# Second feed-forward of a kernel of two transformer blocks: down-projection pieces braided with block pieces of later chunks

## The chip, the cores and the metric

The kernel runs on one core of one Trainium2 chip. Its time is the device time of one launch in microseconds. TensorE (PE) multiplies, VectorE (DVE) and ScalarE (ACT) work elementwise, GpSimd (POOL) does little here, and SyncE (SP) issues the loads.

## The reference, cut to what matters

Two transformer blocks run one after the other on x of 256 tokens by 2048 columns, in float32. The parts that the change touches:

```python
# first block, attention (16 heads, 128 + 64 columns each); the 64 rope columns of k are shared by all heads
q = concat([q[..., :128], apply_rope(q[..., 128:], positions)])
k = concat([k[..., :128], apply_rope(k[..., 128:], positions)])
attn = causal_block_attention(q, k, v)
...
# first block, feed-forward, D_FF = 5632
h2 = rmsnorm(x, ffn_norm_g)
x = x + (silu(h2 @ w_ffn_gate) * (h2 @ w_ffn_up)) @ w_ffn_down
...
# second block, feed-forward, D_FF_2 = 8192
h2 = rms_norm(x, g_ff)
x = x + jnp.square(jax.nn.relu(h2 @ w_ff1)) @ w_ff2
```

## The kernel before

All matrix products run in a split form: an operand is cut into a high part that TensorE takes exactly and a low rest, and a product is three matmuls (high by high, low by high, high by low). Activations are split once and stay in SBUF. Weights come in **pieces** of 512 KB: 256 rows by 512 columns (two k tiles). The function `drive` walks a list of jobs in program order. For each piece it places a load on SP into a raw slot (L197), a cast to the high part on ACT (L230), a subtraction for the low part on DVE (L232), and the piece's matmuls on PE. Casts and subtractions are placed up to `AHEAD` pieces before the matmuls (4 for a PLAIN piece, 3 for MIX and STR), as far as a slot of W for the two parts is free: 6 slots for PLAIN pieces, 3 for MIX, 2 for STR. A load may be issued when the piece that had its raw slot before is split. Each engine runs its instructions in the order in which they were placed, SP too.

A **plain piece** (`chunk`, L262 to L264) is 12 matmuls of 512 columns: 2 k tiles by 2 token tiles by 3. A **block piece** (`strassen`, kind STR, L315 to L317) computes the same product of 2 by 2 blocks from seven block products instead of eight: 21 matmuls of 256 columns. It needs three weight sums beforehand, made on DVE in the raw slot (`sums`, L207 to L209, called L223 to L225 in the kernel after), placed two pieces before the split. Its seven products lie in PSUM banks 0 to 3, and `fin` combines them at the end of a chunk (ACT L328, DVE L329 to L332). Raw slots before: R has 4 for plain pieces of all kinds, G has 3 for block pieces.

Stages in order: the first block's projections and attention (`t_pair` transposes q and k of a pair of heads, `s_pair` makes the scores), its output projection (`wide`, three calls; `transposed_s` transposes the result and forms its block sums), the first feed-forward in three groups (11 gate chunks of plain pieces, each braided with an up chunk of block pieces, and after each group the down chunks), the second block, and the second feed-forward. There, 16 chunks of ff1 (512 columns each, 8 pieces) alternate plain and block: a plain and a block chunk are braided (pieces p p s p s p s p s p s p s p s s), and after each second braid come 32 plain down pieces over 16 k tiles. `ends` applies relu and square to a block chunk (ACT), `t_a` transposes a chunk (PE) and splits it (ACT L378, DVE L379), `ev_acc` adds a down result to x (DVE, L907; L953 after).

Of the kernel before, what the change touches and what calls it, by code (L numbers as in the profile page):

```python
# [24 lines left out]
RAWS = 3  # L25
# [46 lines left out]
def body(tc, d, out):  # L72
# [4 lines left out]
    with tc.manual_schedule(), \  # L77
# [82 lines left out]
        def drive():  # L160
# [3 lines left out]
            seen_h, seen_r, cnt = {}, {}, {}  # L164
            for i, j in enumerate(pcs):
                kind = j[5]

                def cells(s):
                    a, b, w = hslots(s)
                    return [(o + x) // 256 for o in (a, b) for x in range(0, w, 256)]  # L170

                last, s = min((max(seen_h.get(x, -1) for x in cells(s)), s) for s in SLOTS[kind])
                num.append(s)
                free_h.append(last)
                seen_h.update((x, i) for x in cells(s))
                rk = kind == STR
                m = cnt.get(("r", rk), 0)
                cnt[("r", rk)] = m + 1
                slot = (rk, m % (RAWS if rk else RAW))
                rnum.append(slot[1])  # L180
                free_r.append(seen_r.get(slot, -1))
                seen_r[slot] = i
            raws, hl, used = {}, {}, [-1]
            nd, nt, ns = [0], [0], [0]

            def dma():
                while nd[0] < len(pcs) and free_r[nd[0]] < ns[0] and nd[0] < ns[0] + 2 * RAW:
                    i = nd[0]
                    if i in before_dma:
                        before_dma[i]()  # L190
                    src = pcs[i][1]
                    a, n = src.shape[1], src.shape[2]
                    if pcs[i][5] == STR:
                        t = G[:, 2048 + 2048 * rnum[i] : 4096 + 2048 * rnum[i]]
                    else:
                        t = R[:, 1024 * rnum[i] : 1024 * rnum[i] + 1024]
                    sync.dma_start(t[:, : a * n].rearrange("p (a b) -> p a b", a=a), src)  # L197
                    raws[i] = t
                    nd[0] += 1

            def sums(upto):

                while nt[0] <= min(upto, nd[0] - 1):
                    i = nt[0]
                    if pcs[i][5] == STR:
                        v = raws[i].rearrange("p (a b) -> p a b", a=8)
                        dve.tensor_tensor(v[:, 4:6, :], v[:, 0:4:3, :], v[:, 1::-1, :], op=ALU.subtract)  # L207
                        dve.tensor_tensor(v[:, 6, :], v[:, 3, :], v[:, 4, :], op=ALU.subtract)  # L208
                        dve.tensor_tensor(v[:, 7, :], v[:, 2, :], v[:, 6, :], op=ALU.subtract)  # L209
                    nt[0] += 1  # L210

            def split(upto):
                while ns[0] <= min(upto, len(pcs) - 1) and free_h[ns[0]] <= used[0]:
# [9 lines left out]
                    if kind == STR:  # L223
                        n, a = 1792, 7
                        t = t[:, 256:]  # L225
# [16 lines left out]
            for j in jobs:  # L242
                if j[0] == "run":
                    j[1]()
                else:
                    split(k + AHEAD[j[5]])
                    assert ns[0] > k
                    j[2](*hl.pop(k))
                    used[0] = k
                    k += 1  # L250

# [44 lines left out]
        def strassen(pair, forms, w, kts, c0, evict, later=False):  # L296
# [3 lines left out]
            prod = [(("x", 0, 0), 0, 2, 1), (("x", 1, 0), 1, 0, 0), (("s", 3), 2, 3, 0), (("x", 1, 1), 6, 2, 0),  # L300
                    (("s", 0), 3, 1, 1), (("s", 1), 5, 0, 1), (("s", 2), 4, 1, 0)]

            def mk(j):
                def fn(h, l):
                    opened = set()
                    for x, wi, bank, half in prod:
                        o = PS[:, bank * 512 + half * QW : bank * 512 + (half + 1) * QW]
                        if x[0] == "x":
                            xh, xl = pair(2 * j + x[1], x[2])
                        else:  # L310
                            xh, xl = forms[:, 0, j, x[1], :], forms[:, 1, j, x[1], :]
                        first = j == 0 and bank not in opened
                        opened.add(bank)
                        last = j == kts // 2 - 1
                        pe.matmul(o, xh, h[:, wi, :], start=first, stop=False, skip_group_check=True)  # L315
                        pe.matmul(o, xl, h[:, wi, :], start=False, stop=False, skip_group_check=True)  # L316
                        pe.matmul(o, xh, l[:, wi, :], start=False, stop=last, skip_group_check=True)  # L317
                return fn

            for j in range(kts // 2):  # L320
                items.append(piece(wsrc(w, 2 * j, c0, 512), mk(j), kind=STR))

            def fin():
                q = PS[:, 0:2048].rearrange("p (a b) -> p a b", a=8)
                u = rview(G, 1024, 4, QW)
# [3 lines left out]
                dve.tensor_tensor(u[:, 0:2, :], v[:, 0:1, :].to_broadcast(bc), q[:, 0:2, :], op=ALU.add)  # L329
                dve.tensor_tensor(u[:, 2:4, :], u[:, 1:2, :].to_broadcast(bc), q[:, 2:4, :], op=ALU.add)  # L330
                dve.tensor_tensor(v[:, ::-1, :], u[:, 2:3, :].to_broadcast(bc), q[:, 3:5, :], op=ALU.add)
                dve.tensor_tensor(u[:, 3, :], u[:, 3, :], q[:, 6, :], op=ALU.add)  # L332
                if not later:
                    ends()

            def ends():
                evict(0, rview(G, 1024, 4, QW)[:, 0:4:3, :])
# [5 lines left out]
        def braid(a, b, inject=None):  # L343

            pa, pb = [x for x in a if x[0] == "pc"], [x for x in b if x[0] == "pc"]
            order = [pa[0], pa[1]]
            for i in range(6):
                order += [pb[i], pa[i + 2]]
            order += [a[-1], pb[6], pb[7], b[-1]]
            for at in sorted(inject or {}, reverse=True):  # L350
                order.insert(at, ("run", inject[at]))
            return order

        def transposed_s(nat, pair, forms, kts, gain):

            x4, s4 = rview(G, 0, 2, 2, NT, P), rview(G, 1024, 2, 4, P)
# [319 lines left out]
        qkT = rview(B, 4096, 2, 6, S)  # L676
        pT = [rview(B, 4096 + 3072, 2, 512), rview(C, 2048, 2, 512)]
# [5 lines left out]
        def zero_pT():  # L683
            for t in pT:
                pool.memset(t[:, :, 0:P].bitcast(F32), 0.0)

# [34 lines left out]
        def t_pair(p):  # L721
# [12 lines left out]
            split2(qkT[:, 0, 4:6, :], qkT[:, 1, 4:6, :], bank.rearrange("p (a b) -> p a b", a=2))  # L734

        def s_pair(p):
            rq = rqs[p % 2]
            banks = []
            for h in range(2):
                bank = aux_tile()  # L740
                banks.append(bank)
                for qt in range(NT):
# [3 lines left out]
                    hp = slice(64 * h, 64 * h + 64)  # L746
                    mm3(o, [qkT[hp, i, 4, qs] for i in range(2)], [qkT[hp, i, 5, :] for i in range(2)], False, True)
# [91 lines left out]
        def wide(pair, w, ev, tr, pending, kts=16, inject=None, row0=0, last=PLAIN):  # L839

            for c in range(4):
                inj = dict(inject or {}) if c == 0 else {}
                if pending is not None:
# [4 lines left out]
                                  kind=last if c == 3 else PLAIN))  # L848
# [65 lines left out]
        for gi, (c0, nch) in enumerate(groups):  # L914
            aT = pairat(B, 0, 16)
            for j in range(nch):
                c = c0 + j
                jobs.extend(braid(chunk(h2T, "w_ffn_gate", KT, c * 512, 512, ev_silu, kind=MIX, fixed=(4, 5)),
# [279 lines left out]
        def half(tok, i):  # L1198

            v = rview(G, 1024, 4, QW)[:, 0:4:3, :] if tok == 0 else tmp.rearrange("p (a b) -> p a b", a=2)  # L1200
# [10 lines left out]
        pending = {4: pending}  # L1211
        for gi in range(4):
            aT = pairat(B, 0, 16)
            for j in range(0, 4, 2):
                c = 4 * gi + j
                plain = chunk(h2T, "w_ff1_2", KT, c * 512, 512, lambda tok, ps: relu2(abuf[:, tok, :], tok, ps),
                              kind=MIX, fixed=(4, 5))
                block, ends = strassen(h2T, h2F, "w_ff1_2", KT, (c + 1) * 512, lambda tok, v: relu2(v, tok, v), later=True)
                jobs.extend(braid(plain, block, pending))
                pending = {1: t_a(aT, blocks(abuf), j), 2: ends, 7: t_a(aT, half, j + 1)}  # L1220
            for oc in range(4):
                inj = None
                if oc == 0:
                    inj = {1: pending[2], 2: pending[1], 4: pending[7]}
                    pending = None
                ev = ev_out(oc) if gi == 3 else ev_acc(oc)
                jobs.extend(chunk(aT, "w_ff2_2", 16, oc * 512, 512, ev, row0=16 * gi, inject=inj,
                                  kind=MIX, fixed=DOWN[oc]))


# [17 lines left out]
def blockwise(name, c):  # L1248

    return name == "w_ffn_up" or (name == "w_ff1_2" and c % 2 == 1)  # L1250
# [62 lines left out]
```

## Time and profile before

| | us |
|---|---|
| time before, median of 3 runs (lowest, highest) | 2721.99 (2720.91, 2722.18) |
| time of the profiled execution | 2722.61 |
| its span, first to last instruction | 2720.9 |

The profile is of one core at full granted clock. Busy time of an engine is given as a share of the span; a matmul's duration in the profile overlaps the next one's, so that the distance from one start to the next is what a matmul costs.

### The profile page before, as it was taken

How to read it: one execution, taken by the hardware profiler on the slowest of the kernel's cores; microseconds unless marked ns; L12 is line 12 of the kernel's file. 1: busy time of each engine (PE TensorE's matmuls, PEld its weight loads, DVE VectorE, ACT ScalarE, POOL GpSimd, SP SyncE). 2: the span in 40 equal slices, each digit the busy share in tenths (PEclk: the TensorE clock that was granted, in tenths of full speed). 3: DMA queues.
4: the chain of work that ended last, by engine and by line, in shares of the span. 5: the costliest groups of instructions: out<-in, count | busy, mean ns of one | idle time of the engine just before them, and what ended most of it. 6: DMA issues, size and time to landing. Idle time of an engine off the chain costs nothing. (4 is left out here: it accounts for less than half of the span.)

```text
span 2720.9 us, 35965 instructions
## 1 busy us (share of the span) xinstructions
PE 2709.6 (100%) x13996; PEld 2278.4 (84%) x13996; DVE 1851.8 (68%) x2233; ACT 1402.6 (52%) x1749; POOL 73.0 (3%) x153
## 2 busy tenths in 40 slices
PE   9999999999999999999999999999999999999999
PEld 8988888888888888888888888888888888898887
DVE  6555667766996699579755565455678486685774
ACT  6544666545654455345455555544556355464553
POOL 1000111000000000000000010000000000000000
PEclk9999999999999999999999999999999999999999
DMA  7666534554555555565555554555555555655555
GB/s 255 212 212 201 168 127 146 177 180 172 200 187 179 202 206 186 180 210 185 177 196 172 192 183 166 188 188 181 173 180 182 190 200 177 208 179 185 209 176 164
DMA packets 143179, 506.66 MB, mean 186 GB/s; under 512 B 16160, under 2 KB 18592, under 8 KB 142496
## 3 DMA queue, kind: packets, MB, share of 16 engines
q1 hardware_dynamic: 142864, 504.31, 54.8%
q8 instruction: 109, 1.79, 0.3%
q14 instruction: 62, 0.51, 0.1%
q10 hardware_dynamic: 144, 0.05, 0.0%
HBM read 502.21 MB, written 2.10 MB: 185 GB/s over the span
## 5 line engine op out<-in xcount | busy, mean ns | idle before, releaser
L232 DVE TENSOR_TENSOR W<-R,W 128x1024 fp32r<-128x1024 f32 (+2 forms) x795 | 943.5, 1208 | 508.8 <-ACT W L230 505.4
L230 ACT CAST W<-R 128x1024 fp32r<-128x1024 f32 (+2 forms) x798 | 810.7, 1035 | 532.1 <-PE PS L264 445.1
L263 PE MATMUL PS<-W,A 128*128 128x512 f32 (+2 forms) x1728 | 677.8, 392 | 3.2 <-DVE W L232 3.1
L262 PE MATMUL PS<-W,A 128*128 128x512 f32 (+2 forms) x1728 | 678.5, 393 | 0.6 <-ACT W L230 0.4
L264 PE MATMUL PS<-W,A 128*128 128x512 f32 (+2 forms) x1728 | 675.8, 391 | 0.0
L262 PE MATMUL PS<-W,B 128*128 128x512 f32 (+1 forms) x1248 | 492.0, 394 | 0.0
L263 PE MATMUL PS<-W,B 128*128 128x512 f32 (+1 forms) x1248 | 489.4, 392 | 0.9 <-DVE W L232 0.9
L264 PE MATMUL PS<-W,B 128*128 128x512 f32 (+1 forms) x1248 | 489.3, 392 | 0.0
L230 ACT CAST W<-G 128x1792 fp32r<-128x1792 f32 x152 | 257.5, 1694 | 304.7 <-PE PS L316 173.6
L264 PEld LDWEIGHTS PS<-W,A 128*128 128x128 f32 x1728 | 323.9, 187 | 73.7
L263 PEld LDWEIGHTS PS<-W,A 128*128 128x128 f32 x1728 | 324.4, 188 | 72.5 <-DVE W L232 6.6
L262 PEld LDWEIGHTS PS<-W,A 128*128 128x128 f32 x1728 | 324.2, 188 | 68.3 <-ACT W L230 0.8
L232 DVE TENSOR_TENSOR W<-G,W 128x1792 fp32r<-128x1792 f32 x152 | 307.0, 2020 | 40.6 <-ACT W L230 40.6
L263 PEld LDWEIGHTS PS<-W,B 128*128 128x128 f32 x1248 | 234.1, 188 | 54.6 <-DVE W L232 1.8
L264 PEld LDWEIGHTS PS<-W,B 128*128 128x128 f32 x1248 | 233.9, 187 | 54.2
L262 PEld LDWEIGHTS PS<-W,B 128*128 128x128 f32 x1248 | 234.0, 188 | 53.7
L317 PE MATMUL PS<-W,C 128*128 128x256 f32 x608 | 169.8, 279 | 0.0
L315 PE MATMUL PS<-W,C 128*128 128x256 f32 x608 | 169.8, 279 | 0.0
L316 PE MATMUL PS<-W,C 128*128 128x256 f32 x608 | 169.4, 279 | 0.0
L315 PE MATMUL PS<-W,A 128*128 128x256 f32 x456 | 128.6, 282 | 0.0
L317 PE MATMUL PS<-W,A 128*128 128x256 f32 x456 | 127.3, 279 | 0.8 <-DVE W L232 0.8
L316 PE MATMUL PS<-W,A 128*128 128x256 f32 x456 | 127.3, 279 | 0.0
(231 smaller groups left out, 2481.5 us busy)
## 6 DMA issues: line engine op xcount, KB each, us to landing
R<-in_w_in_dram SPq DMA_DIRECT2D x224, 512.0 KB, 4.5
R<-in_w_ff_dram SPq DMA_DIRECT2D x192, 512.0 KB, 3.6
R<-in_w_ffn_gate_dram SPq DMA_DIRECT2D x88, 512.0 KB, 4.4
G<-in_w_ffn_up_dram SPq DMA_DIRECT2D x88, 512.0 KB, 3.5
R<-in_w_ffn_down_dram SPq DMA_DIRECT2D x88, 512.0 KB, 3.5
R<-in_w_out_dram SPq DMA_DIRECT2D x64, 512.0 KB, 4.3
G<-in_w_ff_dram SPq DMA_DIRECT2D x64, 512.0 KB, 3.5
R<-in_w_attn_o_dram SPq DMA_DIRECT2D x32, 512.0 KB, 4.2
```

The source lines that it names most:

```text
L230: act.copy(hv, v)
L232: dve.tensor_tensor(lv, v, hv.bitcast(F32), op=ALU.subtract)
L262: pe.matmul(o, x[0], w[0], start=first, stop=False)
L263: pe.matmul(o, x[0], w[1], start=False, stop=False)
L264: pe.matmul(o, x[1], w[0], start=False, stop=last)
L315: pe.matmul(o, xh, h[:, wi, :], start=first, stop=False, skip_group_check=True)
L316: pe.matmul(o, xl, h[:, wi, :], start=False, stop=False, skip_group_check=True)
L317: pe.matmul(o, xh, l[:, wi, :], start=False, stop=last, skip_group_check=True)
```

## The change

Five parts. (1) In the second feed-forward only ff1 chunks 0 and 1 are plain; chunks 2 to 15 are block chunks. Chunk 1 is braided with chunk 2. Each of chunks 3 to 15 is braided with 8 down pieces of earlier chunks, in the pattern p p s p s p s s twice, so that `down` is cut into 32 chunks over 8 k tiles instead of 16 over 16. Of each such ff1 chunk the piece j = 4 is `flat`: eight products of 256 columns, as a MIX piece, without sums. That makes 99 block pieces for 64. (2) `sums` handles two block pieces in one set of three instructions where the two stand at most six pieces apart and the load of the second has been placed; otherwise one. (3) G has four raw slots of 1792 columns, two neighbours for a pair; `fin`'s result and `transposed_s`'s sums move from G to the last quarter of R, so that MIX pieces have three raw slots (PLAIN pieces four). (4) In `wide`'s calls that end in MIX, chunks 1 to 3 are MIX, not chunk 3 alone. (5) The rope part of the scores is contracted over 128 rows: the k rows of the other head are zeros in two copies of k.

```diff
@@ drive
+RSLOTS = {0: range(4), 1: range(3)}
...
+                if kind == STR:
+                    blocks_at.append(i)
+                    r = 4 + (len(blocks_at) - 1) % 4
+                else:
+                    r = min((seen_r.get(x, -1), x) for x in RSLOTS[kind])[1]
...
+            mate = {}
+            for a, b in zip(blocks_at[0::2], blocks_at[1::2]):
+                if b - a <= 6:
+                    mate[a] = b
@@ sums
-                    if pcs[i][5] == STR:
-                        v = raws[i].rearrange("p (a b) -> p a b", a=8)
-                        dve.tensor_tensor(v[:, 4:6, :], v[:, 0:4:3, :], v[:, 1::-1, :], op=ALU.subtract)
...
+                    if pcs[i][5] == STR and i not in summed:
+                        n = 2 if i in mate else 1
+                        if n == 2:
+                            if mate[i] < nd[0]:
+                                summed.add(mate[i])
+                            elif i > ns[0]:
+                                return
+                            else:
+                                n = 1
+                        o = 1024 + 1792 * (rnum[i] - 4)
+                        v = G[:, o : o + 1792 * n].rearrange("p (c a b) -> p c a b", c=n, a=7)
+                        dve.tensor_tensor(v[:, :, 4:6, :], v[:, :, 0:4:3, :], v[:, :, 1::-1, :], op=ALU.subtract)
+                        dve.tensor_tensor(v[:, :, 6, :], v[:, :, 3, :], v[:, :, 4, :], op=ALU.subtract)
+                        dve.tensor_tensor(v[:, :, 0, :], v[:, :, 2, :], v[:, :, 6, :], op=ALU.subtract)
@@ strassen
+                def flat_fn(h, l):
+                    h, l = (t.rearrange("p a (b c) -> p (a b) c", b=2) for t in (h, l))
+                    for kt, tok, wi, bank, half in flat:
+                        three(at(bank, half), pair(2 * j + kt, tok), h[:, wi, :], l[:, wi, :], False,
+                              (bank, half) == (3, 1) and kt == 1 and j == max(plain))
@@ the order of pieces
+        BRAID, HALF = "ppspspspspspspss", "ppspspss" * 2
@@ t_pair and s_pair
-            split2(qkT[:, 0, 4:6, :], qkT[:, 1, 4:6, :], bank.rearrange("p (a b) -> p a b", a=2))
+            split2(qkT[:, 0, 4, :], qkT[:, 1, 4, :], bank[:, 0:S])
+            for h in range(2):
+                hp = slice(64 * h, 64 * h + 64)
+                split2(qkT[hp, 0, 5 + h, :], qkT[hp, 1, 5 + h, :], bank[hp, S:])
...
-                    mm3(o, [qkT[hp, i, 4, qs] for i in range(2)], [qkT[hp, i, 5, :] for i in range(2)], False, True)
+                    mm3(o, [qkT[:, i, 4, qs] for i in range(2)], [qkT[:, i, 5 + h, :] for i in range(2)], False, True)
@@ wide
-                                  kind=last if c == 3 else PLAIN))
+                                  kind=last if c else PLAIN))
@@ second feed-forward
+        def down(g, oc, fixed):
+            at = 8 * (g % 2)
+            return chunk(Pair(aT.v[:, :, at : at + 8, :]), "w_ff2_2", 8, oc * 512, 512, (ev_out if g == 7 else ev_acc)(oc),
+                         row0=8 * g, kind=MIX, fixed=fixed)
...
+        jobs.extend(at_pieces(ff1(0), {3: pending}))
+        block, ends = ff1_blocks(2)
+        jobs.extend(merge(BRAID, ff1(1), block, {3: t_c(0, blocks(abuf))}))
+        pending = {1: t_c(1, blocks(abuf)), 2: ends, 7: t_c(2, half)}
+        for c in range(3, 16):
+            g, o = (c - 3) // 2, 2 * ((c - 3) % 2)
+            block, ends = ff1_blocks(c, (4,))
+            jobs.extend(merge(HALF, down(g, o, (4, 5)) + down(g, o + 1, (4, 5)), block, pending))
+            pending = {2: ends, 7: t_c(c, half)}
```

**Place 1, DVE in the second feed-forward.** In the rows below W<-R is the subtraction of a plain or flat piece, W<-G that of a block piece, and G<-G with 512 and 256 elements are the sums; DMAHW numbers name the load that a row waits for. Before, in a braid:

```order
L232 TENSOR_TENSOR W<-R,W 128x1024 [waits DMAHW3_49,Activation_49]
L207 TENSOR_TENSOR G<-G 128x512 [waits DMAHW6_49]
L208 TENSOR_TENSOR G<-G 128x256 [waits DVE_49]
L209 TENSOR_TENSOR G<-G 128x256 [waits DVE_49]
L232 TENSOR_TENSOR W<-G,W 128x1792 [waits PE_49,Activation_49]
L232 TENSOR_TENSOR W<-R,W 128x1024 [waits DMAHW5_49,Activation_49]
```

After, in a loop of an odd chunk, from the first down chunk's result (L953, behind piece n5) on; L419 is the transposed chunk's split:

```order
L953 TENSOR_TENSOR X<-X,PS 128x512 [waits PE_49] x2
L247 TENSOR_TENSOR W<-R,W 128x1024 [waits DMAHW3_49,Activation_49]
L419 TENSOR_TENSOR B<-PS,B 128x512 [waits Activation_49] x2
L223 TENSOR_TENSOR G<-G 128x2x512 [waits DMAHW6_49,DMAHW0_49]
L224 TENSOR_TENSOR G<-G 128x2x256 [waits DVE_49]
L225 TENSOR_TENSOR G<-G 128x2x256 [waits DVE_49]
L247 TENSOR_TENSOR W<-R,W 128x1024 [waits DMAHW4_49,Activation_49]
L247 TENSOR_TENSOR W<-R,W 128x1024 [waits DMAHW5_49,Activation_49]
L247 TENSOR_TENSOR W<-G,W 128x1792 [waits Activation_49]
L223 TENSOR_TENSOR G<-G 128x2x512 [waits DMAHW4_49,DMAHW1_49]
```

The set of sums of pieces n12 and n14 now stands between the subtraction of n9 and that of n10, and waits for two loads; the next set, of n15 and the following loop's n2, stands ahead of the subtraction of n13.

**Place 2, SP in the second feed-forward.** Loads in program order; R is a plain or flat piece's raw slot, G a block piece's. Before, in a braid:

```order
L197 DMA R_74<-in_w_ff1_2_dram 128x1024 [waits DMAHW2_49,DVE_49]
L197 DMA G_67<-in_w_ff1_2_dram 128x1024 [waits DMAHW4_49,DVE_49]
L197 DMA R_74<-in_w_ff1_2_dram 128x1024 [waits DMAHW3_49]
L197 DMA G_67<-in_w_ff1_2_dram 128x1024 [waits DMAHW6_49,DVE_49]
L197 DMA R_74<-in_w_ff1_2_dram 128x1024 [waits DMAHW5_49]
```

After, the loads of a loop's pieces n11 to n15 and of the next loop's n0:

```order
L204 DMA R_74<-in_w_ff2_2_dram 128x1024 [waits DMAHW7_49,DVE_49]
L204 DMA G_67<-in_w_ff1_2_dram 128x1024 [waits DMAHW6_49]
L204 DMA R_74<-in_w_ff2_2_dram 128x1024 [waits DMAHW2_49,DVE_49]
L204 DMA G_67<-in_w_ff1_2_dram 128x1024 [waits DMAHW0_49]
L204 DMA G_67<-in_w_ff1_2_dram 128x1024 [waits DMAHW1_49]
L204 DMA R_74<-in_w_ff2_2_dram 128x1024 [waits DMAHW3_49,DVE_49]
```

Before, the loads of block pieces waited for a DVE subtraction, and those of plain pieces were free behind them. Now the loads into R wait for DVE, the loads into G behind them do not.

## Rows read from the trace of the kernel before

**Rows 1.** Profile page, first part: busy us (share of the span) xinstructions of each engine

```profile
PE 2709.6 (100%) x13996; PEld 2278.4 (84%) x13996; DVE 1851.8 (68%) x2233; ACT 1402.6 (52%) x1749; POOL 73.0 (3%) x153
```

**Rows 2.** Waits of PE, whole span: who waited for whom, us, times, longest

```profile
PE PS L263 <- DVE W L232: 4.1, 6, 0.9
```

**Rows 3.** Busy time by stretch: a braid of the first feed-forward

```profile
719.00:762.00 43.00, 43.00 (x272) 38.25 (x271) 40.97 (x49) 23.39 (x22) 0.00 (x0) 1.00 0.57 196
```

**Rows 4.** Timeline of PE, second feed-forward: start us, us, engine, line, operation

```profile
2235.65 0.39 PE L262 MATMUL PS<-W,A 128*128 128x512 f32 x1
...
2238.44 0.28 PE L315 MATMUL PS<-W,A 128*128 128x256 f32 x1
...
2240.89 0.39 PE L262 MATMUL PS<-W,A 128*128 128x512 f32 x1
...
2246.14 0.27 PE L391 MATMUL PS<-cst,G 128*128 128x128 f32 x1
...
2246.94 0.48 PE L262 MATMUL PS<-W,A 128*128 128x512 f32 x1
```

**Rows 5.** Timeline of DVE, end of that braid; in brackets idle time before and releaser

```profile
745.22 2.02 DVE L232 TENSOR_TENSOR W<-G,W 128x1792 fp32r<-128x1792 f32 x1 [1.30 <-ACT W L230]
747.16 0.69 DVE L207 TENSOR_TENSOR G<-G 128x512 f32<-128x512 f32 x1
...
748.68 2.35 DVE L232 TENSOR_TENSOR W<-R,W 128x1024 fp32r<-128x1024 f32 x2
...
752.48 2.02 DVE L232 TENSOR_TENSOR W<-G,W 128x1792 fp32r<-128x1792 f32 x1
754.41 0.68 DVE L329 TENSOR_TENSOR G<-tmp,PS 128x512 f32<-128x512 f32 x1
...
756.97 0.75 DVE L899 SCALAR_TENSOR_TENSOR G<-G,st 128x512 f32<-128x512 f32 x1
...
758.30 1.22 DVE L232 TENSOR_TENSOR W<-R,W 128x1024 fp32r<-128x1024 f32 x1
```

**Rows 6.** Timelines of PE and ACT, the same place

```profile
743.37 0.39 PE L262 MATMUL PS<-W,A 128*128 128x512 f32 x1
751.07 0.40 PE L262 MATMUL PS<-W,A 128*128 128x512 f32 x1
743.49 1.69 ACT L230 CAST W<-G 128x1792 fp32r<-128x1792 f32 x1 [3.56 <-PE PS L316]
```

**Rows 7.** Timeline of DVE: two instructions that read 512 columns of PSUM

```profile
724.26 1.28 DVE L379 TENSOR_TENSOR B<-PS,B 128x512 fp32r<-128x512 f32 x2
```

**Rows 8.** Loads by line: xcount, KB each, median us from issue to landing

```profile
R<-in_w_ffn_gate_dram SPq DMA_DIRECT2D x88, 512.0 KB, 4.4
G<-in_w_ffn_up_dram SPq DMA_DIRECT2D x88, 512.0 KB, 3.5
```

**Rows 9.** Loads of 2254.7 to 2255.2 us: the fourth issued within 1.7 us

```profile
R<-in_w_ff_dram SPq DMA_DIRECT2D x1, 512.0 KB, 5.9
```

**Rows 10.** Waits of SP's queue, whole span: us, times, longest

```profile
SPq L197 <- DVE W L232: 2251.9, 790, 11.4
```

**Rows 11.** Timeline of PE, scores of one pair of heads

```profile
312.51 0.38 PE L262 MATMUL PS<-B 64*128 64x256 f32 x1
312.73 0.28 PE L263 MATMUL PS<-B 64*128 64x256 f32 x1
...
313.61 0.38 PE L262 MATMUL PS<-B 64*128 64x256 f32 x1
```

**Rows 12.** Timeline of PE, last chunk of `wide` before the first feed-forward

```profile
648.51 0.40 PE L262 MATMUL PS<-W,B 128*128 128x512 f32 x1
649.38 0.50 PE L263 MATMUL PS<-W,B 128*128 128x512 f32 x1 [0.47 <-DVE W L232]
```

**Rows 13.** Timelines of DVE and PE, entry into the first braid

```profile
656.12 1.23 DVE L232 TENSOR_TENSOR W<-R,W 128x1024 fp32r<-128x1024 f32 x1 [1.57 <-ACT W L230]
658.40 0.69 DVE L207 TENSOR_TENSOR G<-G 128x512 f32<-128x512 f32 x1 [1.06 <-DMA G<-in_w_ffn_up_dram]
...
663.24 0.40 PE L262 MATMUL PS<-W,A 128*128 128x512 f32 x1
```

More of the change, by code (lines that the diff above doesn't have):

```diff
@@ L306, in fn @@
                     for x, wi, bank, half in prod:
[L307 to L312, printed above, removed]
-                        opened.add(bank)
[L314 to L318, printed above, removed]
+                        xs = pair(2 * j + x[1], x[2]) if x[0] == "x" else [forms[:, i, j, x[1], :] for i in range(2)]
+                        three(at(bank, half), xs, h[:, wi, :], l[:, wi, :], j == 0 and bank not in opened,
+                              j == kts // 2 - 1)
+                        opened.add(bank)
+                def flat_fn(h, l):
[3 more added lines that the diff above has]
+                              (bank, half) == (3, 1) and kt == 1 and j == max(plain))
+                return flat_fn if j in plain else fn
+            assert 0 not in plain and kts // 2 - 1 not in plain
             for j in range(kts // 2):
-                items.append(piece(wsrc(w, 2 * j, c0, 512), mk(j), kind=STR))
+                items.append(piece(wsrc(w, 2 * j, c0, 512), mk(j), kind=MIX if j in plain else STR))
             def fin():
                 q = PS[:, 0:2048].rearrange("p (a b) -> p a b", a=8)
-                u = rview(G, 1024, 4, QW)
                 v = tmp.rearrange("p (a b) -> p a b", a=2)
@@ L341, in strassen, with merge @@
             return (items, ends) if later else items
[L343 to L351, printed above, removed]
+        def merge(pattern, a, b, inject=None):
+            lists, order, n = {"p": list(a), "s": list(b)}, [], 0
+            for c in pattern:
+                if inject and n in inject:
+                    order.append(("run", inject[n]))
+                src = lists[c]
+                order.append(src.pop(0))
+                n += 1
+                while src and src[0][0] == "run":
+                    order.append(src.pop(0))
+            assert not lists["p"] and not lists["s"]
             return order
+        BRAID, HALF = "ppspspspspspspss", "ppspspss" * 2
         def transposed_s(nat, pair, forms, kts, gain):
[L356 removed]
+            x4, s4 = rview(G, 0, 2, 2, NT, P), rview(R, 3072, 2, 4, P)
             for b in range(2):
@@ L1210, in body @@
         stage(MIX)
[L1211 to L1228, printed above, removed]
+        aT = pairat(B, 0, 16)
@@ L1231, in body @@
+        tail = down(6, 2, (4, 5)) + down(6, 3, (0, 1))
+        for oc in range(4):
+            tail += down(7, oc, [(2, 3), (4, 5), (0, 1), (2, 3)][oc])
+        jobs.extend(at_pieces(tail, {2: ends, 5: t_c(15, half)}))
         drive()
```

73 lines of the change are left out of this document (45 added, 28 removed).

## Prediction

> **What bounds it now.** I read the page's busy shares first: PE is busy for the whole span, DVE for 68% [rows 1]. Then the waits of PE: over the kernel it waited for DVE only 4.1 us at its second matmul [rows 2]. So the time is the sum of what matmuls cost, and a change pays by giving PE less, as long as DVE, which prepares the weights, stays ahead. The timeline of PE gives the price of a piece, from start to start: plain 2.80 us (2235.65 to 2238.44), block 2.45 (to 2240.89), eight transposes 0.80 (2246.14 to 2246.94) [rows 4]. By stretches, a braid of 43.0 us has DVE busy for 40.97 [rows 3]: 95%, with no slack to speak of. The timeline of DVE at a braid's end shows how it gets by [rows 5, 6]. PE leaves the block piece n12 at 743.37; ACT casts n15 into the slot then free (743.49), DVE subtracts (745.22) and is free at 747.16: 3.79 us after PE left n12. One set of sums takes 1.52 (747.16 to 748.68), a plain subtraction 1.14 (the pair 2.35, less the overlap), a block subtraction 1.93 (752.48 to 754.41), `fin` 2.56 (to 756.97). `fin` starts 3.34 us after PE has ended n15 (751.07), just early enough for n2 of the next braid.
>
> **The change, part by part.**
>
> *Columns.* 35 more block pieces at 0.35 us less each [rows 4]: -12.3 us. A flat piece has 24 matmuls of 256 columns, and 24/21 of 2.45 is 2.80, as a plain one.
>
> *Rope.* A block of three 128-row and three 64-row matmuls of 256 columns takes 1.10 us (312.51 to 313.61) [rows 11]; at a block piece's 2.45/21 = 0.117 per matmul six would take 0.70. The rest falls where the number of rows changes (0.22 from the first 64-row matmul to the second). 8 pairs have 4 blocks each: 32 x 0.40 = -12.8 us. That all of it goes is a choice; the low end is the half of it at the 64-row side, -6. The two more splits on ACT and DVE in `t_pair` lie beside the next chunk's matmuls.
>
> *Sums by two.* 512 elements take 0.69 us and 1024 take 1.22 [rows 5], 0.53 for 512 more; a pair's three instructions have 1024 more in all, so a pair costs 1.52 + 1.06 = 2.58 against 3.04 for two single sets. DVE per loop then is: 9 plain subtractions 10.3, 7 block 13.5, sums about 9.3, `fin` with a fifth instruction 2.8, two down results and the transposed split at 1.2 each [rows 7] 3.6: 39.5 us against PE's 9 x 2.80 + 7 x 2.45 + 0.80 = 43.15. By busy time it fits. The order decides.
>
> *The loads behind the sums.* A 512 KB load lands 3.5 us after its issue, one issued right behind another 4.4 [rows 8], a fourth in a burst 5.9 [rows 9]: about 1.3 us more for each in front. SP takes loads in order, and practically every one waits for a DVE subtraction [rows 10]. With three raw slots, the load of n13 waits for the subtraction of n9, and n14's stands behind it. But the order on DVE (front, place 1) puts the sums of n12 and n14 right behind n9 and the transposed split, ahead of n10. So DVE stands still until a load that it has itself just released has landed. Before, the sums needed one load, released some 6 us of DVE work earlier (7, sums, 8, 9: 1.14 + 1.52 + 1.93 + 1.14).
>
> I walked two loops by these durations, zero at PE's start of n0. Odd chunk: `fin` ends at 6.3, n3 7.5, sums 6+7 at 10.1, n4 12.1; PE wants n4's low part at 11.2 and **waits 1.0**. n8 and n9 are done at 19.4 and 21.8; loads of n11, n12, n13, n14 go out at 19.5, 19.9, 21.8, 22.2, and the last lands at 26.7. DVE, through with the transposed split at 22.9, idles 3.8; sums 29.3, n10 30.5; PE wants it at 28.8, **waits 1.8**. Then sums 15 + next n2, whose load stands behind that of the next n1, released by n11: idle 3.2, n13 is done at 40.5, PE wants it at 38.8, **waits 1.7**. Then sums of the next loop's n4 + n6: n6's load stands behind n5's, released by n0: idle 2.5. The next n2 is split at 55.0, and `fin` frees bank 3 at 57.4, where PE (n0 at 48.0) wants it at 54.4: **waits 3.0**. Even chunk: sums 7 and 12 are single and their loads early, no wait until the end, where the sums of the next n2 + n4 push the down result behind n0: banks 4 and 5 come free **0.6** late. Two loops cost 1.0 + 1.8 + 1.7 + 3.0 + 0.6 = 8.1 us; of 13 loops seven are odd, and the last odd one has no next: +52 us. Bounds: if a load behind another landed as soon as a single one (1.3 less at three places), two loops cost 4.2 and the term is +26; if each took 5.9 (1.1 more), 11.4 and +73. I take the middle, since both loads go out within 0.4 us as in rows 8.
>
> [...]
>
> *Entries into braids.* Ahead of a braid that follows plain pieces, the sums of n2 + n4 stand before n0's subtraction, and n4's load behind n3's, which waits for the last plain piece. At the first entry that subtraction ends at 657.35 [rows 13]; 4.8 us for the loads, 2.58, then n0's 1.22: 665.9. PE wants it 0.23 after 663.24: a wait of 2.5. Before, DVE waited 1.06 us here for one load, and PE none. Four such entries: +10; I take +8.5, since of the waits of rows 2 some stand there and go.
>
> *`wide`.* PE waited 0.63 us in chunk 3 (0.87 from 648.51 to 649.38 for 0.23) [rows 12], where only three slots lie ahead of `transposed_s`. Chunks 1 and 2 get that too, in two calls: 4 x 0.63 = +2.5, between 0 and 5.
>
> *First feed-forward.* A pair's sums stand before n4 after `fin`: 1.06 us later, while `fin` starts 0.5 earlier. I take +0.2 in 8 braids: +1.5.
>
> **Sum**, against the profiled execution's 2722.6: -12.3 - 12.8 + 52 + 8.5 + 2.5 + 1.5 = +39.4, so 2762; the median of the runs is 0.6 less: **2761 us**, slower by 1.4%. Its own bounds: 2731 (loads at 3.5, in the entries too) to 2787 (loads at 5.9), 2794 with rope at half.
>
> **Rivals.** *DVE keeps ahead, and the change is faster.* Everything hangs on one place: the load of a mate against the 1.2 to 2.3 us of DVE work between its release and the sums. It decides where a mate lands within about 3.0 us of its release, since n10 then comes in time (4.9 less 1.8). Then -12.3 - 12.8 + 2.5 + 1.5 remain, with 1.6 us of order waits in two loops at most (10): 2701 to 2711, say 2706. For it: DVE's 39.5 of 43.15 us is less than in the braids of now, which hardly wait. Against it: no median in rows 8 is below 3.5. Chance 0.16. [...]
>
> *The two cancel.* If a stalled PE gives DVE back more than I walked, the loops cost about 25 and the entries half: 2722.6 - 25.1 + 25 + 4 + 2.5 + 1.5 = 2730, and at +17 no change. Chance for within 0.2% 0.06; the stretch from there to 2735 belongs to my forecast's low end.
>
> *It spreads.* If a load takes 5.9 in the first feed-forward too, sums 10+12 and 6+8 there come late in all 11 braids, at about 1.5 each: 2787 + 16 = 2803. For it: rows 9 are of a stretch with plain pieces alone, where bursts of that length do occur. Against it: a braid of now has one plain piece between two block pieces, and its loads go in pairs, at the 4.4 of rows 8. Chance 0.05.
>
> **Chances.** Forecast 0.73, faster 0.16, no change 0.06, spread 0.05. What a measurement of this kernel tells from no change is about 0.2%, 5.4 us. Faster 0.16, same 0.06, slower 0.78. The range runs from 2721 to 2789: it leaves out the faster case and the spread one.
>
> **What would show it.** Waits of PE at its low-part matmuls (L280 of a plain piece, L329 of a block piece in the kernel after) for DVE of 60 us or so in all, most in the second feed-forward; DVE idle at L223 for loads into G, about 3 us at a time, three times in two loops; loops of 48 and 46.5 us by turns; score blocks of 0.70 us. If DVE at L223 waits for nothing, or PE's waits stay near 4 us, I am wrong at the loads. If loops are evenly long, the walk is wrong though the cause may be right.

## The result and the profile after

The changed kernel took 2829.27 us (median of 4 runs, 2826.39 to 2832.53) against 2722.09 (2720.91 to 2723.05): ratio 1.0394, interval [1.0376, 1.0412]. Slower, as forecast, but by 107 us where the forecast had 39, and above the range (2721 to 2789).

The page of the profiled execution (2828.3 us), engines and their busy time, beside [rows 1]:

```profile
span 2826.6 us, 36849 instructions
...
PE 2727.7 (97%) x14467; PEld 2315.3 (82%) x14467; DVE 1935.6 (68%) x2162; ACT 1427.7 (51%) x1771; POOL 74.0 (3%) x155
```

PE is no longer busy all the time, and DVE's share is what it was. The waits of PE, over the kernel (waiting engine, line, what it waited for: us in total, times, longest), where [rows 2] had 4.1 us:

```profile
PE PS L329 <- DVE W L247: 33.4, 27, 3.1
PE PS L280 <- DVE W L247: 27.8, 18, 4.0
PE PS L327 <- DVE tmp L358: 17.6, 6, 5.0
PE PS L279 <- ACT G L1241: 7.3, 1, 7.3
PE PS L279 <- ACT W L245: 4.4, 8, 1.1
```

L329 and L280 want a low part, L327 a bank that `fin` frees. DVE's own waits, by line and by what ended them, show what it stood at:

```profile
DVE G L223 <- DMA G<-in_w_ff_dram: 94.5, 31, 8.5
...
DVE G L223 <- DMA G<-in_w_ffn_up_dram: 36.1, 20, 6.0
...
DVE G L223 <- issue: 14.7, 5, 4.2
```

L223 is the first instruction of the sums. Loads ended 131 us of its waits (94.5 and 36.1); for the other 14.7 ("issue") the profile names nothing that ended them. In the second feed-forward all five stand at one place of the loop, where a sixth loop waits for a load. One such place in the second feed-forward, in the timeline of DVE (start, duration, what it is, in brackets the idle time ahead and what ended it):

```profile
2122.84 1.22 DVE L247 TENSOR_TENSOR W<-R,W 128x1024 fp32r<-128x1024 f32 x1
2123.98 1.28 DVE L419 TENSOR_TENSOR B<-PS,B 128x512 fp32r<-128x512 f32 x2
2130.04 1.23 DVE L223 TENSOR_TENSOR G<-G 128x1024 f32<-128x1024 f32 x1 [4.78 <-DMA G<-in_w_ff_dram]
2131.30 0.69 DVE L224 TENSOR_TENSOR G<-G 128x512 f32<-128x512 f32 x1
...
2132.63 2.35 DVE L247 TENSOR_TENSOR W<-R,W 128x1024 fp32r<-128x1024 f32 x2
2134.90 2.02 DVE L247 TENSOR_TENSOR W<-G,W 128x1792 fp32r<-128x1792 f32 x1
2140.87 1.22 DVE L223 TENSOR_TENSOR G<-G 128x1024 f32<-128x1024 f32 x1 [3.95 <-DMA G<-in_w_ff_dram]
```

SP's timeline shows that the loads go out together, five in 3 us, the moment the subtractions before have freed slots:

```profile
2121.76 0.33 SPq L204 DMA_DIRECT2D R<-in_w_ff_dram  x1
2122.14 0.42 SPq L204 DMA_DIRECT2D G<-in_w_ff_dram  x1
2124.09 0.33 SPq L204 DMA_DIRECT2D R<-in_w_ff_dram  x1
2124.47 0.90 SPq L204 DMA_DIRECT2D G<-in_w_ff_dram  x2
2133.88 1.46 SPq L204 DMA_DIRECT2D R<-in_w_ff_dram  x2
```

The DMA view of 2122 to 2150 gives the rate in 40 slices of 0.7 us, and the medians from issue to landing ([rows 8] had 3.5 for `in_w_ffn_up`):

```profile
GB/s 0 217 304 380 404 410 410 269 257 410 392 234 59 0 0 0 0 0 146 187 404 293 357 310 357 181 35 0 0 0 0 0 0 47 140 357 410 427 117 0
...
G<-in_w_ff_dram SPq DMA_DIRECT2D x5, 512.0 KB, 5.4
```

Bursts at 410 GB/s with nothing between. The five loads from 2121.76 on landed 3.5, 4.4, 3.8, 5.5 and 6.3 us after they were issued. The fourth is that of n14, the second piece of the set: its 5.5 us end at 2129.97, and the sums start at 2130.04. And PE, in the same stretch:

```profile
2131.06 0.28 PE L328 MATMUL PS<-W,A 128*128 128x256 f32 x1
2133.91 0.38 PE L329 MATMUL PS<-W,A 128*128 128x256 f32 x1 [2.56 <-DVE W L247]
...
2144.74 0.50 PE L280 MATMUL PS<-W,B 128*128 128x512 f32 x1 [2.52 <-DVE W L247]
...
2147.12 0.63 PE L279 MATMUL PS<-W,B 128*128 128x512 f32 x1
2147.54 0.63 PE L280 MATMUL PS<-W,B 128*128 128x512 f32 x1
```

Two waits of 2.5 us, 11 us apart, and then matmuls of 512 columns start 0.43 us apart instead of 0.23 for some 3 us (granted clock 0.53 from 2146.0 to 2149.6). The view by stretches (us; busy of PE, PEld, DVE, ACT, POOL; granted clock; DMA share; GB/s) shows it in the clock's column, the first row away from the second feed-forward, the others in it:

```profile
200.00:400.00 200.00, 200.00 (x1000) 169.76 (x999) 123.32 (x218) 116.49 (x237) 18.30 (x28) 1.00 0.50 166
...
2130.00:2150.00 20.00, 14.91 (x83) 12.88 (x82) 15.87 (x14) 7.81 (x6) 0.00 (x0) 0.91 0.40 138
...
2200.00:2400.00 200.00, 181.91 (x1098) 160.87 (x1097) 157.16 (x156) 96.88 (x92) 0.00 (x0) 0.97 0.48 169
2400.00:2600.00 200.00, 180.62 (x1079) 159.67 (x1078) 155.59 (x154) 97.27 (x92) 0.00 (x0) 0.96 0.48 169
```

To see where all of it lies, I took from the timeline of PE each matmul's distance to the next, less what it takes undisturbed (0.2333 us for 512 columns, 0.1167 for 256), and summed what is over. The columns of the table are stretches of the span in us, the same for all kernels, so that the entry of the second feed-forward falls before 2040 in some and after it in others. The lower rows are runs that are explained below:

| | 0-530 | 530-670 | 670-1345, first ff | 1345-2040 | from 2040, second ff | sum |
|---|---|---|---|---|---|---|
| before | 15.5 | 0.7 | 4.3 | 3.4 | -0.1 | 23.8 |
| after | 10.8 | 7.3 | 22.5 | 3.0 | 98.7 | 142.3 |
| single sums | 8.6 | 2.7 | 4.9 | 10.7 | 16.6 | 43.5 |
| early block loads | 10.3 | 2.1 | 6.6 | 5.0 | 40.1 | 64.1 |
| pairs by age | 8.6 | 2.1 | 6.6 | 5.0 | 15.8 | 38.1 |
| single, old slots | 8.7 | 0.7 | 4.2 | 3.6 | 16.3 | 33.5 |
| three plain first | 4.2 | 0.7 | 4.4 | 3.6 | 6.5 | 19.4 |

The table closes: 142.3 - 23.8 and the -12.3 forecast for fewer columns make +106.2, and the two profiled executions differ by 105.7.

### The profile page after: what moved, and what is told of

It is laid out like the page before. It is cut to its first block, busy times and chain, and to the rows that moved or that the text cites. A ratio compares the mean times of both kernels' runs of the same rounds, so it can differ in the third digit from the quotient of the medians.

```text
span 2826.6 us, 36849 instructions
## 1 busy us (share of the span) xinstructions
PE 2727.7 (97%) x14467; PEld 2315.3 (82%) x14467; DVE 1935.6 (68%) x2162; ACT 1427.7 (51%) x1771; POOL 74.0 (3%) x155
## 4 chain that ended last, share of the span: by engine, by line
PE 68%; DVE 17%; DMA 6%; issue 4%; ACT 4%; SPq 0%; DVEq 0%; ACTq 0%
PE PS L280 19%; PE PS L281 19%; PE PS L279 19%; DVE W L247 8%; DMA G<-in_w_ff_dram 4%; PE PS L329 3%; PE PS L327 3%; PE PS L328 3%; DVE G L223 3%; ACT W L245 2%; DMA G<-in_w_ffn_up_dram 2%; DVE G L224 1%; PE PS L431 1%; DVE X L953 1%; SPq L204 0%
## 5 line engine op out<-in xcount | busy, mean ns | idle before, releaser
L247 DVE TENSOR_TENSOR W<-R,W 128x1024 fp32r<-128x1024 f32 (+2 forms) x760 | 899.9, 1206 | 395.5 <-ACT W L245 392.6
L245 ACT CAST W<-R 128x1024 fp32r<-128x1024 f32 (+2 forms) x763 | 771.6, 1034 | 460.9 <-PE PS L281 344.8
L280 PE MATMUL PS<-W,A 128*128 128x512 f32 (+2 forms) x1536 | 604.2, 393 | 11.6 <-DVE W L247 11.6
L279 PE MATMUL PS<-W,A 128*128 128x512 f32 (+2 forms) x1536 | 605.6, 394 | 8.5 <-ACT G L1241 7.3
L281 PE MATMUL PS<-W,A 128*128 128x512 f32 (+2 forms) x1536 | 602.9, 393 | 0.0
L245 ACT CAST W<-G 128x1792 fp32r<-128x1792 f32 x187 | 316.3, 1691 | 460.9 <-DVE G L225 255.1
L280 PE MATMUL PS<-W,B 128*128 128x512 f32 (+1 forms) x1248 | 492.7, 395 | 16.3 <-DVE W L247 16.3
L247 DVE TENSOR_TENSOR W<-G,W 128x1792 fp32r<-128x1792 f32 x187 | 377.1, 2019 | 68.7 <-ACT W L245 68.7
L280 PEld LDWEIGHTS PS<-W,A 128*128 128x128 f32 x1536 | 290.4, 189 | 73.8 <-DVE W L247 13.9
L279 PEld LDWEIGHTS PS<-W,A 128*128 128x128 f32 x1536 | 289.8, 189 | 70.6 <-ACT G L1241 8.0
L281 PEld LDWEIGHTS PS<-W,A 128*128 128x128 f32 x1536 | 289.9, 189 | 66.0
L280 PEld LDWEIGHTS PS<-W,B 128*128 128x128 f32 x1248 | 235.6, 189 | 70.5 <-DVE W L247 20.8
L329 PE MATMUL PS<-W,A 128*128 128x256 f32 x665 | 193.7, 291 | 33.4 <-DVE W L247 33.4
L223 DVE TENSOR_TENSOR G<-G 128x1024 f32<-128x1024 f32 (+1 forms) x100 | 115.3, 1153 | 145.6 <-DMA G<-in_w_ff_dram 94.5
L327 PE MATMUL PS<-W,C 128*128 128x256 f32 x748 | 211.1, 282 | 0.0
L329 PE MATMUL PS<-W,C 128*128 128x256 f32 x748 | 211.1, 282 | 0.0
L328 PE MATMUL PS<-W,C 128*128 128x256 f32 x748 | 210.5, 281 | 0.0
L327 PE MATMUL PS<-W,A 128*128 128x256 f32 x665 | 192.7, 290 | 17.6 <-DVE tmp L358 17.6
```

The source lines that it names most:

```text
L223: dve.tensor_tensor(v[:, :, 4:6, :], v[:, :, 0:4:3, :], v[:, :, 1::-1, :], op=ALU.subtract)
L245: act.copy(hv, v)
L247: dve.tensor_tensor(lv, v, hv.bitcast(F32), op=ALU.subtract)
L279: pe.matmul(o, x[0], w[0], start=first, stop=False)
L280: pe.matmul(o, x[0], w[1], start=False, stop=False)
L281: pe.matmul(o, x[1], w[0], start=False, stop=last)
```

## Experiments

Eleven kernels, in three sets. The expectations call them by their place in a set: single sums, early block loads, single sums with old slots, rope alone; then bank order, pairs by age, extra subtractions, bank order with rope casts; then three plain first, rope casts alone, pairs by age with three plain first. Line numbers differ by a few between kernels.

**Single sums.** The theory: with a pair DVE waits for a load that it has itself just released, and PE behind it. Rivals: the order of nine plain and seven block pieces is too dense for DVE anyway; or the raw slot that was taken away holds the loads back.

```
-                if b - a <= 6:
-                    mate[a] = b
+                pass
```

> The kernel after with every set of sums made for one block piece (no mates), nothing else changed. In the trace of the kernel after, PE stands still or runs slowly for 89 us in the loops of the second feed-forward, 18 us more than before in the first one and 7.5 us ahead of the first braid of the second. Theory (DVE, with a pair's sums, waits for a load that it has itself just released, and PE for DVE behind it): a single set waits only for its own load, so most of this goes: 2735 us (2715 to 2755), DVE at L223 waits under 40 us in all instead of 145. Rival 1 (the order of nine plain and seven block pieces is too dense for DVE by itself): 2800 or more, and DVE has its busy share of the loops rise to 85%. Rival 2 (the raw slot that was taken away, three instead of four, holds the loads back whatever is summed): 2780 or more, with DVE still waiting for loads into G for 80 us or more.

2729.53 us, 1.0025 [1.0016, 1.0035]; granted clock 0.998. 100 us come back with nothing else touched. DVE's waits for loads into G are 35 us (26.6 for `in_w_ff`, 8.6 for `in_w_ffn_up`) instead of 131, though the page has a load of `in_w_ff` into G land as late as in the kernel after (5.3 us, there 5.4):

```profile
DVE G L222 <- DMA G<-in_w_ff_dram: 26.6, 16, 6.6
...
G<-in_w_ff_dram SPq DMA_DIRECT2D x99, 512.0 KB, 5.3
```

So the time from issue to landing does not decide alone: it costs where an instruction that stands in front of others waits for that load. Rivals 1 and 2 are out as main cause.

**Early block loads.** Sums by two as in the kernel after, but block loads go out in a line of their own.

```
-                while nd[0] < len(pcs) and free_r[nd[0]] < ns[0] and nd[0] < ns[0] + 2 * RAW:
-                    i = nd[0]
+            line = [[i for i, j in enumerate(pcs) if (j[5] == STR) == k] for k in (False, True)]
...
+                while ready(line[0]) or ready(line[1]):
+                    q = min((q for q in line if ready(q)), key=lambda q: q[0])
+                    i = q.pop(0)
```

> The kernel after, sums still by two, but the loads of block pieces are issued in an order of their own: a block piece's load goes out as soon as its own raw slot is free, no longer behind the loads of plain pieces that wait for theirs. Theory (the pair's second load is late because it stands behind a plain piece's load): PE's waits in the loops fall from 65 us to under 20 and the half clock behind them with it: 2725 us (2705 to 2750). Rival (the pair's set itself, 2.58 us of DVE work ahead of a subtraction that is due, makes PE wait whenever its loads come): 2790 or more, with DVE's wait at L223 gone and PE's waits still there.

2748.52 us, 1.0095 [1.0080, 1.0111]. 81 of the 107 us are gone, yet not all, so neither side had it whole. DVE's timeline shows what is left:

```profile
2125.52 2.02 DVE L252 TENSOR_TENSOR W<-G,W 128x1792 fp32r<-128x1792 f32 x1
2130.66 1.23 DVE L228 TENSOR_TENSOR G<-G 128x1024 f32<-128x1024 f32 x1 [3.12 <-DMA G<-in_w_ff_dram]
```

and SP's, when that load went out:

```profile
2126.01 0.42 SPq L210 DMA_DIRECT2D G<-in_w_ff_dram  x1
```

4.65 us from issue to sums, and issued while the block subtraction ahead of the sums ran. Once in two loops the second load's own slot comes free this late.

**Pairs by age.** To tell the late load from the long set: the same, but a pair is formed only where the second load was issued two splits earlier.

```
-                            if mate[i] in raws:
+                            if mate[i] in raws and born[mate[i]] < ns[0] - 1:
                                 summed.add(mate[i])
-                            elif i > ns[0]:
-                                return
                             else:
                                 n = 1
```

> The second run's kernel (sums by two, block loads in an order of their own), but two sets are made together only where the second piece's load was issued at least two splits earlier; otherwise the set is made for one piece at once. That kernel still lost 20 us in waits for low parts and 12 in slow matmuls, and its DVE waited 3.1 us once in two loops for a load whose raw slot had only just come free. Theory (only a load that was just released costs; the long set by itself does not): 2725 us (2716 to 2735). Rival (the 2.58 us set ahead of a subtraction that is due): 2742 or more, and DVE's wait at the sums gone.

2725.80 us, 1.0013 [1.0004, 1.0022]. The groups of DVE by line and shape, of the kernel after:

```profile
L223 DVE TENSOR_TENSOR G<-G 128x1024 f32<-128x1024 f32 x87 | 106.3, 1222 | 135.5 <-DMA G<-in_w_ff_dram 84.4 <-DMA G<-in_w_ffn_up_dram 36.1 <-issue 14.7
...
L223 DVE TENSOR_TENSOR G<-G 128x512 f32<-128x512 f32 x13 | 8.9, 688 | 10.1 <-DMA G<-in_w_ff_dram 10.1
```

and of this run:

```profile
L227 DVE TENSOR_TENSOR G<-G 128x1024 f32<-128x1024 f32 x87 | 106.0, 1218 | 7.9 <-DMA G<-in_w_ff_dram 5.7 <-DMA G<-in_w_ffn_up_dram 2.2
...
L227 DVE TENSOR_TENSOR G<-G 128x512 f32<-128x512 f32 x13 | 8.9, 682 | 0.0
```

87 pairs and 13 single sets in both, at the same 1.22 us: in one kernel DVE stands idle for 146 us ahead of them, 131 of these ended by loads, in the other for 8, and the time differs by 103. The pair as such is cleared of the loss.

**Single sums and the old slots.** Beside single sums, four raw slots for plain pieces, three for blocks, `fin`'s scratch in G, and `wide` as before (`last if c == 3 else PLAIN`).

> As the first of these, single sums, and also the slots of the kernel before (four raw slots for plain pieces, three for blocks, fin's scratch back in G) and the wide projection's chunks 1 and 2 with four pieces ahead: what is left of the change is the new order of the second feed-forward and the rope scores. Theory: the slots add little once no pair waits, 2 to 10 us under the first run, of which 2.5 are the wide projection: 2722 us (2705 to 2745). Rival 2 (raw slots): 30 us or more under the first run.

2720.10 us, 0.9992 [0.9983, 1.0002]. 9.4 under the first run: the table has them ahead of the first feed-forward (2.0, `wide`) and ahead of the second (7.1, of which 4.4 are PE's wait for the first chunk's result, on which more below; with the old slots that wait is under 1). What is left of a loss lies in the loops, 13.1 us of it in one row of PE's waits:

```profile
PE PS L323 <- DVE tmp L354: 13.1, 12, 1.1
```

**Another order of banks**, against that wait: the block piece's seven products take bank 0 first.

```
-            prod = [(("x", 0, 0), 1, 2, 1), (("x", 1, 0), 2, 0, 0), ...
+            prod = [(("x", 1, 0), 2, 0, 0), (("s", 1), 6, 0, 1), (("s", 0), 4, 1, 1), (("s", 2), 5, 1, 0), ...
```

> The third run's kernel (single sums, old slots) with the seven products of a block piece in another order: first the two of bank 0, then banks 1, 2 and 3, where it was banks 2, 0, 3, 2, 1, 0, 1. What that kernel still loses in the second feed-forward is one wait of 1.1 us in each of 12 loops, 13.1 in all, of the first block piece for fin's third instruction, which is the one that frees banks 1 and 2; bank 0 is free 1.4 us earlier, with its first. Theory: the wait goes, and a second one of up to 0.4 per loop may come at bank 1: 2709 us (2705 to 2714). Rival (fin as a whole is late, and bank 3, wanted seventh, is late now): 2715 or more.

2720.99 us, 0.9993 [0.9983, 1.0003]: a miss, the rival is right in kind. The wait for `fin` shrank to 4.3 and others took its place, so that the second feed-forward's sum stayed at 16.1:

```profile
PE PS L323 <- DVE tmp L354: 4.3, 12, 0.4
...
PE PS L325 <- DVE W L243: 2.8, 13, 0.4
```

**Rope alone**, in the kernel before.

> The kernel before with the rope scores over 128 rows alone. The sum of the prediction had -12.8 us: 2709. In the trace of the kernel after, a pair's 24 score matmuls take 2.87 us from first start to last for 4.28 of before, but in the last two pairs PE waits for the rope splits on ACT and DVE, 2.3 us, and 2.4 for the softmax: if these come from the two more splits, 2713 to 2715; if they are the wide changes of the kernel after, 2709. If half of the gain is lost, 2716.

2715.20 us, 0.9976 [0.9966, 0.9985]: -7.2. The timeline of DVE in the next to last pair:

```profile
470.30 0.41 DVE L379 TENSOR_TENSOR B<-PS,B 128x256 fp32r<-128x256 f32 x1
471.14 0.42 DVE L379 TENSOR_TENSOR B<-PS,B 64x256 fp32r<-64x256 f32 x1 [0.43 <-ACT B L378]
471.99 0.43 DVE L379 TENSOR_TENSOR B<-PS,B 64x256 fp32r<-64x256 f32 x1 [0.43 <-ACT B L378]
```

and of ACT:

```profile
466.66 0.38 ACT L378 CAST B<-PS 128x256 fp32r<-128x256 f32 x1
470.74 0.37 ACT L378 CAST B<-PS 64x256 fp32r<-64x256 f32 x1 [3.71 <-DVE B L379]
471.59 0.37 ACT L378 CAST B<-PS 64x256 fp32r<-64x256 f32 x1 [0.48 <-DVE B L379]
```

The three splits run in turn over two engines, and each cast waits for the subtraction ahead of it. With the casts issued first:

```
+            for hp, m, src in parts:
+                act.copy(qkT[hp, 0, m, :], src)
+            for hp, m, src in parts:
+                dve.tensor_tensor(qkT[hp, 1, m, :], src, qkT[hp, 0, m, :].bitcast(F32), op=ALU.subtract)
```

> The first kernel of this set, and in the rope part the three casts are issued ahead of the three subtractions, the 64-row halves first. In the run of rope alone, the last two pairs have PE wait 2.3 us for these splits, which run in turn: cast, subtraction, cast, subtraction. Theory: 1 to 2.5 us less than the first kernel of this set, 2707 us (2703 to 2712). Rival (the wait is for ACT, which is then behind by the same): no difference.

2715.05 us, 0.9974 [0.9963, 0.9984], 5.9 less than without, more than expected: the softmax wait behind it went too. And in the kernel before:

> The kernel before with the rope scores over 128 rows and the three casts ahead of the three subtractions. Rope alone gave 2715.2. Theory: the full -12.8 of the prediction's term, 2709 us (2707 to 2712). Rival: the casts gave something only beside the rest of the changed kernel: 2714 or more.

2710.25 us, 0.9955 [0.9943, 0.9968]: -11.9, nearly the whole term.

**Extra subtractions**, to see what a wait of PE costs beside its length.

```
+                        for _ in range(1 + again.get(i, 0)):
                             dve.tensor_tensor(lv, v, hv.bitcast(F32), op=ALU.subtract)
...
+            again.update({n0 + 4: 2, n0 + 10: 3})
```

> The third run's kernel, with the subtraction of the fifth piece of each of the 13 loops made three times and that of the eleventh four times (the same result each time): 3.9 and 3.4 us more of DVE work at the two places where PE waited 2.7 us in the kernel after, with no late load in it. This asks what a wait of PE costs beside its own length. In the kernel after, 65 us of waits came with 25 us of matmuls at half clock. If waits bring the half clock, whatever makes them: waits of some 60 us and a granted clock under 0.99, 2795 us (2775 to 2815). If the half clock belongs to the loads or the pairs: clock 0.998, waits alone, 2780 or less.

2805.86 us, 1.0308 [1.0293, 1.0323]; granted clock 0.984 in all, 0.93 in the loops:

```profile
2066.00:2300.00 234.00, 211.60 (x1255) 188.65 (x1254) 220.42 (x243) 113.32 (x111) 0.00 (x0) 0.93 0.45 162
2300.00:2600.00 300.00, 272.11 (x1605) 242.02 (x1605) 282.72 (x313) 142.11 (x134) 0.00 (x0) 0.93 0.46 164
```

DVE waits under 4 us for loads here, as without the edit. Of the 86 us over the kernel without it (single sums with old slots), waits of more than 0.5 us in the second feed-forward make 48.5 (63.5 against 15.0) and slow matmuls, which start 0.02 to 0.5 late, 36.5 (38.8 against 2.3). Of the two places only the fifth piece made PE wait, 3.7 us in each of the 13 loops; the work added at the eleventh made no wait. Behind each of these waits matmuls run slowly for some 5 us (from 2186 to 2191 at a granted clock of 0.50), which costs 2.2 to 2.6 us more. So here the lower clock came behind waits of PE with no late load and no pair about (0.93 in the loops, for 1.00 from 2066 to 2700 in the kernel without the added work).

**Three plain pieces first.** In the kernel with single sums, old slots and the rope casts:

```
-        BRAID, HALF = "ppspspspspspspss", "ppspspss" * 2
+        BRAID, HALF = "ppspspspspspspss", "pppspsspspspspss"
```

> The third run's kernel (single sums, old slots) with the rope casts ahead of their subtractions, and in each loop of the second feed-forward three down pieces ahead of the first block piece, where it was two (order of 16 pieces: pppspsspspspspss). What that kernel loses in the loops is 15 us, 13.1 of them at the first block piece, behind fin, which on DVE stands behind the block subtraction and the sums of that piece. Now a plain subtraction stands there, and PE wants the banks 2.8 us later. Theory: the wait goes, and the columns' -12.3 show: 2720.1 less 6 for the rope casts less 12: 2702 us (2699 to 2708). Rival (the DVE work of a loop is short by as much wherever it is due, and the wait only moves, as it did with the banks in another order): 2712 or more.

2705.39 us, 0.9938 [0.9926, 0.9951]: faster than before by 16.8 us, and than the rope casts alone in the kernel before by 4.9. The loops hold 6.5 us of waits and slow starts instead of 16.3. The table closes here too: 19.4 - 23.8 - 12.3 is -16.7.

**Pairs by age, three plain first**, with the rope casts too, to ask what sums by two are worth without their wait:

> The kernel with pairs by age (sums by two where the second load was issued at least two splits earlier, block loads in an order of their own, three raw slots) with the same two edits as the first kernel of this set. It asks whether sums by two are worth anything once they cost no wait. By age alone it was 2725.8, of which the rope casts should take 6 and the loops some 8: 2712 us (2705 to 2718); the first kernel of this set, single sums and four raw slots, is then 5 to 15 us faster. Rival (the DVE time that pairs save, about 0.46 us each, is what the loops lack): as fast as the first kernel of this set, or faster.

2717.11 us, 0.9983 [0.9974, 0.9992]: 11.7 us behind the single sums with four raw slots. So the DVE time that pairs save brought this kernel no lead. How much of the 11.7 the three raw slots, `wide` (2.5) and the pairs have each was not taken apart, and so it is not shown what the pairs would be worth beside four raw slots.

## Why the prediction was right about the sign and wrong about the size

*Columns, -12.3*: not run alone. Both sums of the table use it, and both close within 0.5 us.

*Rope, -12.8*: the matmuls are as priced (in the kernel after a block of six takes 0.70 us, from 311.91 to 312.61), but that the two more splits "lie beside the next chunk's matmuls" does not hold for the last two pairs: in the run of rope alone PE waits there for the splits (from 470.65 and from 495.05 on, 2.3 us in all) and then for the softmax (2.0). Alone it was worth 7.2.

*The loops, +52: the term that failed.* Mechanism and most places are the predicted ones: sums of n12 and n14 behind n9 and the transposed split, idle 4.78 (walk: 3.8) and at the next set 3.95 (3.2); PE waits 2.73 (1.8) at n10, 2.68 (1.7) at n13, 2.0 to 5.1 (3.0) at `fin`, and the pattern repeats after two loops. Two steps went wrong. First, the walk gave the second load of a set 4.5 us; as the fourth of five that leave in 3 us it took 5.5. DVE also waited in the even loops, where the walk had no load wait: 1.3 to 2.6 us at the single set of n12, and PE up to 1.2 behind it. In all, PE's waits over 0.5 us came to 64.6. That is over 52, but inside the bounds of +26 and +73 that the prediction gave the term. Second, the walk priced a matmul behind a wait like any other and so put the clock at nothing: matmuls that start late by 0.02 to 0.5 us behind those waits add 25 us. Together some 90, which no bound of the term reached. (The bounds themselves go by loads 1.3 us faster and 1.1 slower than walked; 3.5 and 5.9 of the rows against the walk's 4.5 are 1.0 and 1.4, and "1.3 us more for each in front" does not follow from 3.5, 4.4 and 5.9. With 1.4 the upper end would be some 6 us higher, still far short.)

*Entries, +8.5*: 3.56, 3.70 and 2.82 at three of them (2.5 each predicted), and the fourth is 7.45, on a path that the walk leaves out. PE at the entry of the second feed-forward's first braid:

```profile
2050.13 0.39 PE L281 MATMUL PS<-W,A 128*128 128x512 f32 x1
2057.82 0.80 PE L279 MATMUL PS<-W,A 128*128 128x512 f32 x1 [7.29 <-ACT G L1241]
```

ACT, which has to clear banks 4 and 5:

```profile
2055.49 1.69 ACT L245 CAST W<-G 128x1792 fp32r<-128x1792 f32 x1 [6.39 <-DVE G L225]
2057.08 0.68 ACT L1241 ACTIVATE G<-PS,st 128x512 f32<-128x512 f32 x1
```

The first chunk's result stands on ACT behind the cast of n2, that behind the pair's sums, and those had waited 8.46 us for a load. The same cause by a second engine: 17.5 in all. But the pair is only part of it at this place: with single sums and the same raw slots PE still waits 4.4 here, behind a wait of DVE of 6.6 for one load, and with the old slots under 1.

*`wide`, +2.5*: right (four times 0.63). *First feed-forward, +1.5*: 22.5 less the 4.3 of before and the two entries there is 11.7. "It spreads" was the rival that said so, at 16, with a chance of 0.05; DVE did wait 36.1 us for loads of `in_w_ffn_up` (16 of them at the three entries), which land at a median of 4.5 now, for 3.5 before.

The measured time is 68 us beyond the forecast. The loops' waits make 13 of that and the clock behind them 25, the entries 9, the first feed-forward 10 and the rope splits, as the run of rope alone has them, 6; some 5 us are left over.

"DVE keeps ahead" fell to rows 8, which the prediction had held against it. Where the second load is out early (pairs by age) the loss goes, and the time is within 0.13% of before; the 2706 of that rival does not come. In the kernel after one operation on 1024 elements (1.22 us) costs less than two on 512 (0.69 each), but 87 pairs without waits stand only 3.7 us ahead of single sums with the same three raw slots, whose loads keep one line, and 5.7 us behind single sums with the old slots.

## What to carry to other kernels

An instruction made larger by joining two inputs waits for the later of its inputs, and everything behind it on its engine waits too (at the place shown above the sums stood 4.78 us for a load, and PE 2.56 for a subtraction behind them; over the kernel after the 87 pairs stood 120.5 us for loads, with pairs by age 8); before joining, look at when the second input's load is released, and join only where it is long out. An engine with no slack should be walked with loads in the bunches in which they really leave. And a wait of the matmul engine can cost more than its length: in these runs waits of 3.7 us cost 2.2 to 2.6 more, while waits of 1.1 us cost nothing more.

## What was not expected of the hardware

Behind most of PE's waits of over 2 us in the kernel after (16 of 21) the granted clock soon fell (starts 0.43 us apart at 512 columns instead of 0.23) for 2.5 to 5.5 us, with matmuls on both sides of the wait. In the stretch shown above it fell behind the second of two waits of 2.5 us, 11 us apart. A second wait was not needed: at one entry of the first feed-forward a single wait, with no other longer than 0.6 us in the 120 us before it (granted clock 1.00 from 1087 to 1207), was enough.

```profile
1207.60 0.79 PE L280 MATMUL PS<-W,A 128*128 128x512 f32 x1 [2.66 <-DVE W L247]
...
1208.61 0.63 PE L279 MATMUL PS<-W,A 128*128 128x512 f32 x1
1209.04 0.63 PE L280 MATMUL PS<-W,A 128*128 128x512 f32 x1
```

The granted clock from 1207 to 1211 is 0.57. Waits of such lengths were not always followed by it: in the kernel with early block loads five of the six waits of 2.4 to 3.6 us in the loops were followed by slow matmuls, and the one at 2318 was not. In sum, 65 us of waits came with 25 of late starts in the kernel after, and 48.5 us of added waits with 36.5 in the extra subtractions. The twelve waits of 1.1 us in the loops of single sums with old slots brought none (granted clock 1.00 from 2066 to 2700). Behind the second of the waits of 2.5 us shown above the clock reads 0.50 from 2147 to 2149, as it does from 2186 to 2191 behind a wait of 3.7 us in the extra subtractions. Why some waits of 2 to 3 us were followed by it and others were not, these runs do not show.
